# The small unit of the first feed-forward half step as a plain product with k outermost, PSUM banks of the units swapped, and the rotary angle tables computed in thirty short pieces

## The chip, the core and the metric

The kernel is one program on one core of a Trainium2 chip. The metric is the device time of one execution in microseconds (us), the median of several runs. TensorE (PE) multiplies, VectorE (DVE) and ScalarE (ACT) do elementwise work, GpSimd (POOL) a little of it, and SyncE (SP) issues the DMAs. Each engine works through its own instructions in the order of the program; between engines there are only semaphores.

## What is computed

Two layers, each of a feed-forward half step, a mixing block (attention and pooling) and a second feed-forward half step, on 512 tokens of 1024 channels in float32, then a final norm:

```python
def swiglu(h, w_gate, w_up, w_down):
    return (jax.nn.silu(h @ w_gate) * (h @ w_up)) @ w_down      # 1024 -> 2816 -> 1024

for l in range(2):
    x = x + 0.5 * swiglu(rmsnorm(x, ffn1_norm[l]), ffn1_w_gate[l], ffn1_w_up[l], ffn1_w_down[l])
    ...                                                          # mixing block with partial rotary attention
    x = x + 0.5 * swiglu(rmsnorm(x, ffn2_norm[l]), ffn2_w_gate[l], ffn2_w_up[l], ffn2_w_down[l])
return rmsnorm(x, final_norm)
```

The rotary part needs a table of cosines and sines of the positions, once for the whole program.

## The kernel before, in words

The residual x lies transposed in eight tiles x0 to x7 of 128 channels by 512 tokens; "chunk c" is tile c. Every float32 operand of a product is split into a high part (made by ACT as a rounded copy) and a low part (made by DVE as the difference), and each product is three matmuls: high by high, low by high, high by low. For the weights these parts are called `whi` and `wlo` (L357, L360), for chunk c of the normed input `ah` and `al` (L433, L434 for chunks 0 to 3, L439, L446 for 4 to 7).

A feed-forward half step (`ffn`) works through six units of its 2816 hidden channels: `UNITS = (5, 0, 1, 2, 3, 4)`, a small one of 256 channels first, then five large ones of 512. Of each unit `products` computes gate and up, and one unit later `down` multiplies the result into x. The gate and up product of a unit is done by a seven-product scheme on 2 by 2 blocks (`PORD = (1, 2, 6, 5, 7, 3, 4)`): instead of eight block products there are seven, in return for sums of weight blocks on DVE (`total`, `across`, `every`; L254, L258, L262, L266), sums of the outputs (`evacuate`), and sums and differences of input blocks (`fold`, L447 to L450, split in L453 to L458). Products 1, 2 and 4 take the input blocks themselves, products 6, 5, 7 and 3 the sums. For the small unit a matmul has 256 columns (168 matmuls), for a large one 512.

The order around the change is written by hand. `take` hands out the split weights of a step ("job") and first emits the split of the job two ahead, `divide`. `flush` emits the DVE halves that were put off. At the start, `startup` folds the eight chunks as they arrive and splits the first weights; the squares for the norm are emitted inside products 1 and 2 of the small unit (L662). Later norms come by `Norm.chunk`, called after each output tile of the last `down` or of the mixing block's residual (L937), which folds and squares it. `finish_col` closes a norm: four matmuls with a column of ones (L495), one DVE instruction, one power on POOL (L498). Then `activation_block` applies the gate (ACT L592, DVE L593).

PSUM has eight banks, two each under the tags A, B, C and D. In unit number n of a half step (n counts from 0, the small unit is n = 0) the tiles `px` take tag "AB"[n % 2] and the tiles `pz` the other. `down` uses C, transposes and norms use D. The mixing block's last output tiles, d = 0 to 7, take "AABBCCAA"[d].

The rotary tables are a generator, `tables` (L149). In the first half step of the first layer it is advanced once after each step numbered 6 or later of units n = 1 and n = 2 (L683), in seven pieces, all of which fall into n = 1.

Of the kernel before, what the change touches and what calls it, by code (L numbers as in the profile page):

```python
# [16 lines left out]
P = 128  # L17
# [61 lines left out]
def trunk(ctx: ExitStack, tc: tile.TileContext, a: dict):  # L79
# [39 lines left out]
    def startup(norm):  # L119
# [8 lines left out]
        for c in range(1, 4):  # L128
            nc.sync.dma_start(x[c], a["xT"][c])
        load()  # L130
        for c in range(4, KD):
            nc.sync.dma_start(x[c], a["xT"][c])
        pump()
        nc.sync.dma_start(ident, a["ident"])
# [6 lines left out]
        for c in range(KD):  # L141
            norm.fold(c)
            if c < 2:
                divide(c)
            if c == 4:
                divide()
            flush()

    def tables():  # L149
# [11 lines left out]
        def reduce(t):  # L161
            nearest(k, t, 1.0 / TWO_PI)
            for c in (C1, C2, C3):
                add_times(t, k, -c)
# [3 lines left out]
        nc.vector.tensor_scalar(ang, ang, col[:, 0:1], None, op0=ALU.mult)  # L168
        nearest(far, ang, 2.0**-17)
        add_times(ang, far, -2.0**17)  # L170
        yield
        reduce(ang)
        yield
        turn = t2([P, S], F32, "turn")
        nc.vector.tensor_scalar(turn, far, M1, None, op0=ALU.mult)
        reduce(turn)
        yield
        add_times(turn, far, M2)
        add_times(turn, far, M3)
        reduce(turn)  # L180
        yield
        nc.vector.tensor_tensor(ang, ang, turn, op=ALU.add)
        reduce(ang)
# [6 lines left out]
        nc.vector.tensor_tensor(k, k, k, op=ALU.mult)  # L190
        nc.vector.tensor_scalar(cosT, k, -2.0, 1.0, op0=ALU.mult, op1=ALU.add)
# [109 lines left out]
    def ffn_jobs(i, l):  # L301
        for n, u in enumerate(UNITS):
            pj = product_jobs(i, l, u)
# [105 lines left out]
    class Norm:  # L409
# [11 lines left out]
        def fold(self, c):  # L421

            H = S // 2
            if c == 0:
                self.xs, self.ah, self.al, self.sh, self.sl = ([None] * 4 for _ in range(5))
# [3 lines left out]
            if c < 4:  # L429
# [5 lines left out]
                                                             op=ALU.subtract))  # L435
                return
# [27 lines left out]
        def block(self, p, c, i):  # L464
# [5 lines left out]
            return tuple(t[c][:, z, i * P:(i + 1) * P] for t in (hi, lo))  # L470

# [112 lines left out]
    def ffn(which, l, norm, nxt, first=False):  # L584
# [20 lines left out]
        def products(n, u):  # L605
            N = S if u < NU else S // 2
            w, cps = N // 2, 2 if u < NU else 1
            xs = [bank("AB"[n % 2], f"px_{nm}_{u}_{i}") for i in range(2)]
# [485 lines left out]
```

## Time and profile before

| | before |
|---|---|
| median of 3 runs | 1922.75 us (1921.74 to 1922.85) |
| profiled execution, its own time | 1919.58 us |
| its span in the profile | 1917.8 us |
| TensorE busy | 1857.2 us (97% of the span) |
| VectorE busy | 1444.4 us (75%) |
| ScalarE busy | 950.4 us (50%) |
| GpSimd busy | 116.9 us (6%) |
| DMA | mean 101 GB/s |

TensorE is busy nearly all the time, so what can be won lies in its 60 us of idle time and in the stretches in which its clock is at the lower level. A busy share is a mean over stages with different limits; the stages that the change touches are the start, the first three large units of the first layer, and the three later places where a half step begins. The page's slices show TensorE below nine tenths only in the first three of forty.

### The profile page before, as it was taken

Reading aid. Unit: us, or ns where it says so; the run is one execution under the profiler, and the core shown is the slowest. Engines: PE = TensorE matmul, PEld = TensorE weight load, DVE = VectorE, ACT = ScalarE, POOL = GpSimd, SP = SyncE. Lnnn points to the kernel's source line nnn. Section 1 sums busy time; section 2 is a strip of 40 time slices with the busy share of each in tenths; the row PEclk is TensorE's granted clock in tenths of the full one; section 3 lists DMA queues with packets and bytes.
Section 4 is the critical chain, followed back from the end, with each engine's and each line's share of the span. In section 5 each row is a group of like instructions: output and inputs, shape, how many; then the busy total and the mean of one; then the engine's idle time right before and its main releaser. Section 6 shows DMA issues by size and latency. Waiting matters only on the chain.

```text
span 1917.8 us, 23563 instructions
## 1 busy us (share of the span) xinstructions
PE 1857.2 (97%) x8966; PEld 1551.3 (81%) x8966; DVE 1444.4 (75%) x2041; ACT 950.4 (50%) x1474; POOL 116.9 (6%) x105
## 2 busy tenths in 40 slices
PE   6989999999999999999989999999999989999998
PEld 5868888898877888888878888888888778888887
DVE  6996677647887986778688777675688688777675
ACT  6444344436665553444464444444476565444444
POOL 0000000013230000000000000000323200000000
PEclk7999999999999999999999999999999999999999
DMA  5223333125451233422313322340454223232321
GB/s 183 88 79 100 128 110 107 64 76 145 113 158 56 66 121 99 132 96 97 105 50 116 121 88 88 99 148 17 126 134 126 89 94 116 99 99 96 102 77 45
DMA packets 59696, 194.36 MB, mean 101 GB/s; under 512 B 7920, under 2 KB 8064, under 8 KB 59584
## 3 DMA queue, kind: packets, MB, share of 16 engines
q1 hardware_dynamic: 59440, 192.57, 31.9%
q8 instruction: 70, 1.15, 0.2%
q0 software_dynamic: 144, 0.29, 0.1%
q14 instruction: 42, 0.34, 0.1%
HBM read 171.87 MB, written 2.10 MB: 91 GB/s over the span
## 4 chain that ended last, share of the span: by engine, by line
PE 86%; DVE 8%; ACT 2%; issue 2%; DMA 1%; POOL 1%; SPq 0%; DVEq 0%; POOLq 0%; ACTq 0%
PE pd_f L384 8%; PE pd_f L383 8%; PE pd_f L382 8%; PE px_f L658 8%; PE px_f L655 8%; PE px_f L657 8%; PE pz_f L655 6%; PE pz_f L658 6%; PE pz_f L657 6%; PE pv_m L747 3%; PE ps_m L814 2%; PE pt_m L827 2%; PE pt_f L600 2%; DVE wlo L360 1%; PE po_m L843 1%
## 5 line engine op out<-in xcount | busy, mean ns | idle before, releaser
L360 DVE TENSOR_TENSOR wlo<-raw,whi 128x1024 fp32r<-128x1024 f32 (+2 forms) x421 | 502.0, 1198 | 55.4 <-ACT whi L357 50.4
L357 ACT ACTIVATE whi<-raw 128x1024 fp32r<-128x1024 f32 (+2 forms) x421 | 421.7, 1026 | 220.3 <-DVE wlo L360 63.9
L384 PE MATMUL pd_f<-ah_f,wlo 128*128 128x512 f32 (+1 forms) x736 | 282.2, 383 | 3.1 <-DVE wlo L360 3.1
L382 PE MATMUL pd_f<-ah_f,whi 128*128 128x512 f32 (+1 forms) x736 | 281.5, 382 | 1.0 <-ACT ah_f L400 1.0
L383 PE MATMUL pd_f<-al_f,whi 128*128 128x512 f32 (+1 forms) x736 | 280.7, 381 | 1.0 <-DVE al_f L403 1.0
L708 DVE SCALAR_TENSOR_TENSOR x<-pd_f,x 128x512 f32<-128x512 f32 x184 | 127.0, 690 | 168.8 <-PE pd_f L384 165.5
L592 ACT ACTIVATE c_f<-c_f,rcol_n 128x256 f32<-128x256 f32 (+1 forms) x144 | 70.3, 492 | 272.4 <-DVE c_f L637 102.5
L384 PEld LDWEIGHTS pd_f<-ah_f,wlo 128*128 128x128 f32 x736 | 138.7, 188 | 33.5 <-DVE wlo L360 7.7
L383 PEld LDWEIGHTS pd_f<-al_f,whi 128*128 128x128 f32 x736 | 138.8, 189 | 28.8 <-DVE al_f L403 2.3
L655 PE MATMUL px_f<-whi,ah_n 128*128 128x512 f32 (+1 forms) x384 | 145.9, 380 | 15.7 <-DVE x L937 11.5
L382 PEld LDWEIGHTS pd_f<-ah_f,whi 128*128 128x128 f32 x736 | 138.9, 189 | 27.4 <-ACT ah_f L400 1.9
L655 PE MATMUL px_f<-whi,sh_n 128*128 128x512 f32 (+1 forms) x384 | 144.1, 375 | 5.7 <-ACT c_f L622 5.7
L658 PE MATMUL px_f<-wlo,ah_n 128*128 128x512 f32 (+1 forms) x384 | 145.2, 378 | 1.2 <-DVE wlo L360 1.2
L658 PE MATMUL px_f<-wlo,sh_n 128*128 128x512 f32 (+1 forms) x384 | 144.1, 375 | 1.9 <-DVE wlo L360 1.9
L658 PE MATMUL pz_f<-wlo,sh_n 128*128 128x512 f32 (+1 forms) x384 | 143.3, 373 | 2.1 <-DVE wlo L360 2.1
L657 PE MATMUL px_f<-whi,al_n 128*128 128x512 f32 (+1 forms) x384 | 145.3, 378 | 0.0
L655 PE MATMUL pz_f<-whi,sh_n 128*128 128x512 f32 (+1 forms) x384 | 143.7, 374 | 0.6 <-DVE c_f L624 0.3
L657 PE MATMUL px_f<-whi,sl_n 128*128 128x512 f32 (+1 forms) x384 | 143.7, 374 | 0.0
L657 PE MATMUL pz_f<-whi,sl_n 128*128 128x512 f32 (+1 forms) x384 | 143.1, 373 | 0.0
L819 ACT ACTIVATE e_m<-e_m,nmx_m 128x512 f32<-128x512 f32 x96 | 69.4, 723 | 78.7 <-DVE nmx_m L817 78.1
L655 PEld LDWEIGHTS px_f<-whi,ah_n 128*128 128x128 f32 x384 | 74.3, 193 | 30.1 <-DVE x L937 11.9
L817 DVE CUSTOM_DVE_ANT_0 e_m<-ps_m,gbias 128x512 f32<-128x512 f32 x96 | 65.9, 686 | 33.8 <-PE ps_m L814 33.3
(206 smaller groups left out, 3580.4 us busy)
## 6 DMA issues: line engine op xcount, KB each, us to landing
raw<-in_gu SPq DMA_DIRECT2D x160, 512.0 KB, 3.3
raw<-in_dn SPq DMA_DIRECT2D x80, 512.0 KB, 3.3
raw<-in_wqk SPq DMA_DIRECT2D x24, 512.0 KB, 5.4
qq_m<-hl_q_m SPq DMA_DIRECT2D x48, 256.0 KB, 4.2
raw<-in_wo SPq DMA_DIRECT2D x16, 512.0 KB, 5.3
raw<-in_gs SPq DMA_DIRECT2D x15, 512.0 KB, 4.9
raw<-in_wv SPq DMA_DIRECT2D x16, 384.0 KB, 3.1
kk_m<-hl_k_m SPq DMA_DIRECT2D x48, 128.0 KB, 2.3
```

Of the source, the lines that this page charges most:

```text
L357: nc.scalar.activation(hi[:, o:e], raw[:, o:e], AF.Copy)
L360: nc.vector.tensor_tensor(lo[:, o:e], raw[:, o:e], hi[:, o:e].bitcast(F32), op=ALU.subtract)
L382: nc.tensor.matmul(ps, hi[:, o:o + P], act[0], start=start, stop=False)
L383: nc.tensor.matmul(ps, hi[:, o:o + P], act[1], start=False, stop=False)
L384: nc.tensor.matmul(ps, lo[:, o:o + P], act[0], start=False, stop=stop)
L592: nc.scalar.activation(c[:, :w], src[:, :w], AF.Silu, scale=r)
L655: nc.tensor.matmul(ps, bh, hi[:, o], start=(k == 0 and p in (1, 2, 5)), stop=False, skip_group_check=True)
L657: nc.tensor.matmul(ps, bl, hi[:, o], start=False, stop=False, skip_group_check=True)
L658: nc.tensor.matmul(ps, bh, lo[:, o], start=False, stop=(k == 3), skip_group_check=True)
L708: nc.vector.scalar_tensor_tensor(x[d], ps, 0.5, x[d], op0=ALU.mult, op1=ALU.add)
L817: nc.vector.tensor_tensor_reduce(e, ps, gbias[:, o:o + S], -0.125, 3.0e38, ALU.add, ALU.min, nmx[hd][:, it:it + 1])
L819: nc.scalar.activation(e, e, AF.Exp, bias=nmx[hd][:, it:it + 1], scale=-1.0, accum_out=den[hd][:, it:it + 1])
```

## The change

The gate and up product of the small unit (n = 0) of the first half step, in both layers, becomes a plain product: a new function `plain_unit` with four PSUM tiles of 128 tokens (tags A, A, B, B), input chunk k outermost, 512 columns per matmul, 96 matmuls. Its weights come as four plain jobs of two k slices each. `Norm.fold` makes two more parts, `a2`, of the second half of chunks 0 to 3 for it (one ACT and one DVE instruction of 256 columns each). The bank tags of units are swapped in all half steps. At the start the loads are put in the order in which k needs them, and the squares are emitted in the fold loop. The tables yield after nearly every DVE instruction or pair, and are advanced after every step from number 2 on of n = 1, 2 and 3.

```diff
-        for c in range(1, 4):
+        nc.sync.dma_start(x[1], a["xT"][1])
+        nc.sync.dma_start(x[2], a["xT"][2])
+        load(2)
+        nc.sync.dma_start(x[3], a["xT"][3])
+        for c in range(4, KD):
+            if c % 2 == 0:
+                load()
             nc.sync.dma_start(x[c], a["xT"][c])
...
         for c in range(KD):
             norm.fold(c)
-            if c < 2:
-                divide(c)
-            if c == 4:
-                divide()
+            if c < 4:
+                divide(c % 2)
             flush()
+            if c > 0:
+                norm.square(c - 1)
+        norm.square(KD - 1)
...
         def reduce(t):
             nearest(k, t, 1.0 / TWO_PI)
-            for c in (C1, C2, C3):
-                add_times(t, k, -c)
+            yield
+            add_times(t, k, -C1)
+            yield
+            add_times(t, k, -C2)
+            yield
+            add_times(t, k, -C3)
+            yield
...
     def ffn_jobs(i, l):
         for n, u in enumerate(UNITS):
+            if i == 1 and u == NU:
+                for g in range(4):
+                    plain(("c", l, g), a["gc"][l, g], D)
+                continue
...
+                if self.n % 3 == 0:
+                    a2 = t2([P, 2, H], F32R, f"a2_{nm}")
+                    self.a2[k] = a2
+                    nc.scalar.activation(a2[:, 0, :], xs[:, 1, :], AF.Copy)
+                    later.append(lambda: nc.vector.tensor_tensor(a2[:, 1, :], xs[:, 1, :], a2[:, 0, :].bitcast(F32),
+                                                                 op=ALU.subtract))
...
-            xs = [bank("AB"[n % 2], f"px_{nm}_{u}_{i}") for i in range(2)]
+            xs = [bank("BA"[n % 2], f"px_{nm}_{u}_{i}") for i in range(2)]
...
-                    zs.update({i: bank("BA"[n % 2], f"pz{p}_{nm}_{u}_{i}") for i in range(2)})
+                    zs.update({i: bank("AB"[n % 2], f"pz{p}_{nm}_{u}_{i}") for i in range(2)})
...
-                    if first and not n and p in (1, 2):
-                        for k in range(4 * p - 4, 4 * p):
-                            norm.square(k)
-                            flush()
...
-                    if first and n in (1, 2) and z >= 6:
+                    if first and n in (1, 2, 3) and z >= 2:
                         next(rotary, None)
...
+        def plain_unit(u):
+
+            ps = [bank("AABB"[t], f"pc_{nm}_{t}") for t in range(4)]
+
+            def part(t, k, w, o):
+                ah, al = norm.tile_of(t, k)
+                hi, lo = (v[:, o:o + S] for v in w)
+                nc.tensor.matmul(ps[t], ah, hi, start=(k == 0), stop=False)
+                nc.tensor.matmul(ps[t], al, hi, start=False, stop=False)
+                nc.tensor.matmul(ps[t], ah, lo, start=False, stop=(k == KD - 1))
+
+            for g in range(3):
+                flush()
+                w = take("c", l, g)
+                for z in range(2):
+                    for t in range(4):
+                        part(t, 2 * g + z, w, z * S)
+                    flush()
+            w = take("c", l, 3)
+            norm.finish_col()
+            cs = [t2([P, S], F32, f"cc_{nm}_{t}") for t in range(4)]
+            for t in range(4):
+                for z in range(2):
+                    part(t, 6 + z, w, z * S)
+                flush()
+                activation_block(cs[t], ps[t], t, S // 2)
+            for j in range(2):
+                turns.append(lambda j=j: turn(u, j, cs, j, S // 2))
...
-            products(n, u)
+            if n == 0 and which == 1:
+                plain_unit(u)
+            else:
+                products(n, u)
```

The first place is VectorE at the start. Of the names, `al_n_3` is the low part of chunks 3 and 7, `s_n` and `sl_n` are the sums of the seven-product scheme and their low parts, `sq_n` the squares of the norm, `wlo` the low parts of weights. After the change, from the last fold on, its instructions stand so:

```order
39 L469 TENSOR_TENSOR al_n_3_175<-xs_n_7_236,ah_n_3_174 128x512
40 L470 TENSOR_TENSOR s_n_7_239<-xs_n_3_172,xs_n_7_236 128x256
41 L471 TENSOR_TENSOR s_n_7_240<-s_n_7_239,xs_n_3_172 128x256
42 L472 TENSOR_TENSOR s_n_7_239<-xs_n_3_172 128x256
43 L473 TENSOR_TENSOR s_n_7_240<-xs_n_7_236,s_n_7_240 128x256
44 L480 TENSOR_TENSOR sl_n_6_223<-s_n_6_221,sh_n_6_222 128x512
45 L481 TENSOR_TENSOR sl_n_6_223<-s_n_6_220,sh_n_6_222 128x512
46 L512 TENSOR_TENSOR sq_n_0_155<-sq_n_0_155,sq_n_5_234 128x512
47 L480 TENSOR_TENSOR sl_n_7_242<-s_n_7_240,sh_n_7_241 128x512
48 L481 TENSOR_TENSOR sl_n_7_242<-s_n_7_239,sh_n_7_241 128x512
49 L512 TENSOR_TENSOR sq_n_0_155<-sq_n_0_155,sq_n_6_253 128x512
50 L512 TENSOR_TENSOR sq_n_0_155<-sq_n_0_155,sq_n_7_255 128x512
```

Directly behind these come the low parts of the third and fourth weight job of the plain unit (k = 4 to 7), which TensorE needs next, and two more:

```order
51 L377 TENSOR_TENSOR wlo_267<-raw_99,whi_266 128x1024
52 L377 TENSOR_TENSOR wlo_303<-raw_103,whi_302 128x1024
53 L377 TENSOR_TENSOR wlo_333<-raw_108,whi_332 128x1024
54 L377 TENSOR_TENSOR wlo_363<-raw_110,whi_362 128x1024
55 L529 TENSOR_SCALAR rcol_n_371<-ms_n_366 128x4
```

Before the change the same stretch of VectorE held sums of weight blocks, and the squares came after the folds:

```order
30 L446 TENSOR_TENSOR al_n_3_155<-xs_n_7_204,ah_n_3_154 128x512
31 L447 TENSOR_TENSOR s_n_7_207<-xs_n_3_152,xs_n_7_204 128x256
32 L448 TENSOR_TENSOR s_n_7_208<-s_n_7_207,xs_n_3_152 128x256
33 L449 TENSOR_TENSOR s_n_7_207<-xs_n_3_152 128x256
34 L450 TENSOR_TENSOR s_n_7_208<-xs_n_7_204,s_n_7_208 128x256
35 L457 TENSOR_TENSOR sl_n_6_194<-s_n_6_192,sh_n_6_193 128x512
36 L458 TENSOR_TENSOR sl_n_6_194<-s_n_6_191,sh_n_6_193 128x512
37 L254 TENSOR_TENSOR raw_84<-raw_84,raw_102 128x1024
38 L258 TENSOR_TENSOR sum_5_0_227<-raw_84,raw_104 128x1024
39 L457 TENSOR_TENSOR sl_n_7_210<-s_n_7_208,sh_n_7_209 128x512
40 L458 TENSOR_TENSOR sl_n_7_210<-s_n_7_207,sh_n_7_209 128x512
41 L360 TENSOR_TENSOR wlo_230<-sum_5_0_227,whi_229 128x1024
```

The squares have moved in among the folds, the weight sums are gone, and the weights of k = 4 to 7 stand behind the whole of both.

The second place is VectorE in the first large unit of the first layer (n = 1), around the low parts of the weights of steps 5 and later (`wlo`; x is written by `down`). Before the change a reduction stood as one block (`kmul`, `ang`):

```order
101 L360 TENSOR_TENSOR wlo_704<-raw_279,whi_703 128x1024
102 L708 SCALAR_TENSOR_TENSOR x_66<-pd_f_5_2_731,x_66 128x512
103 L360 TENSOR_TENSOR wlo_727<-raw_371,whi_726 128x1024
104 L708 SCALAR_TENSOR_TENSOR x_67<-pd_f_5_3_740,x_67 128x512
105 L155 TENSOR_SCALAR kmul<-ang 128x512
106 L156 TENSOR_SCALAR kmul<-kmul 128x512
107 L159 SCALAR_TENSOR_TENSOR ang<-kmul,ang 128x512 x3
108 L360 TENSOR_TENSOR wlo_754<-raw_615,whi_753 128x512
```

After the change the first pieces stand between earlier weight splits, one at a time (`far` is a table tile too):

```order
68 L377 TENSOR_TENSOR wlo_470<-sum_0_0_432,whi_469 128x1024
69 L279 TENSOR_TENSOR raw_112<-raw_112,sum_0_0_432 128x1024
70 L176 CAST ang<-pos_i 128x512
71 L177 TENSOR_SCALAR ang<-ang,col 128x512
72 L377 TENSOR_TENSOR wlo_497<-sum_0_1_473,whi_496 128x1024
73 L279 TENSOR_TENSOR raw_114<-raw_114,sum_0_1_473 128x1024
74 L656 TENSOR_TENSOR c_f_0_0_447<-pz_f_0_0_475,c_f_0_0_447 128x512
75 L656 TENSOR_TENSOR c_f_0_1_449<-pz_f_0_1_476,c_f_0_1_449 128x512
76 L159 TENSOR_SCALAR far<-ang 128x512
77 L160 TENSOR_SCALAR far<-far 128x512
78 L377 TENSOR_TENSOR wlo_520<-raw_335,whi_519 128x512
79 L163 SCALAR_TENSOR_TENSOR ang<-far,ang 128x512
```

Two pieces now stand ahead of the split of the first `down` weights (`wlo_520`), where before none did; by the end of this unit twelve pieces are done, and the rest follows in n = 2 and n = 3.

## Rows read from the trace of the kernel before

**Rows 1.** Chain that ended last: transposes opening each unit (start us, us, what).
```profile
60.65 0.87 PE pt_f L600 x8
...
120.40 0.88 PE pt_f L600 x8
...
1006.76 0.87 PE pt_f L600 x8
...
1056.66 0.87 PE pt_f L600 x8
```
**Rows 2.** Timeline, TensorE: where units begin (start us, us, engine, line, what).
```profile
55.02 0.40 PE L655 MATMUL px_f<-whi,ah_n 128*128 128x512 f32 x1
...
968.84 0.28 PE L655 MATMUL px_f<-whi,ah_n 128*128 128x256 f32 x1
...
1001.13 0.40 PE L655 MATMUL px_f<-whi,ah_n 128*128 128x512 f32 x1
```
**Rows 3.** Stretches: us, busy us (instructions) of PE, PEld, DVE, ACT, POOL; PEclk.
```profile
46.38:55.02 8.64, 8.64 (x75) 8.64 (x73) 6.13 (x12) 5.00 (x9) 0.00 (x0) 1.00 0.12 31
55.02:60.49 5.47, 5.47 (x27) 4.46 (x25) 5.22 (x7) 2.86 (x4) 0.00 (x0) 1.00 0.02 3
103.73:106.29 2.56, 2.56 (x8) 1.98 (x6) 2.42 (x5) 0.00 (x0) 0.00 (x0) 0.50 0.00 0
624.85:628.47 3.62, 3.62 (x18) 3.62 (x18) 3.59 (x9) 1.56 (x4) 0.00 (x0) 0.50 0.00 0
20.51:23.78 3.27, 1.23 (x3) 0.79 (x3) 3.23 (x8) 2.39 (x5) 0.00 (x0) 0.60 0.56 213
```
**Rows 4.** Timeline, ScalarE at the start: one chunk, the next, chunk 4, squares.
```profile
8.81 0.72 ACT L428 ACTIVATE xs_n<-x,vecs 128x512 f32<-128x512 f32 x1 [1.34 <-DMA x<-in_xT]
...
9.57 0.42 ACT L433 ACTIVATE ah_n<-xs_n 128x256 fp32r<-128x256 f32 x1
...
9.89 0.61 ACT L357 ACTIVATE whi<-raw 128x512 fp32r<-128x512 f32 x1
...
10.41 0.71 ACT L428 ACTIVATE xs_n<-x,vecs 128x512 f32<-128x512 f32 x1
...
12.61 0.72 ACT L428 ACTIVATE xs_n<-x,vecs 128x512 f32<-128x512 f32 x1
...
30.53 2.17 ACT L474 ACTIVATE sq_n<-x 128x512 f32<-128x512 f32 x4
```
**Rows 5.** Timeline, VectorE: chunk 4's low part, a weight sum, table pieces, a split.
```profile
14.03 0.69 DVE L446 TENSOR_TENSOR al_n<-xs_n,ah_n 128x512 fp32r<-128x512 f32 x1 [0.94 <-ACT ah_n L439]
...
968.95 1.22 DVE L254 TENSOR_TENSOR raw<-raw,raw 128x1024 f32<-128x1024 f32 x1
...
86.18 2.15 DVE L159 SCALAR_TENSOR_TENSOR ang<-kmul,ang 128x512 f32<-128x512 f32 x3
...
1017.76 0.68 DVE L360 TENSOR_TENSOR wlo<-raw,whi 128x512 fp32r<-128x512 f32 x1
```
**Rows 6.** Chain that ended last: the norm's four products on TensorE, one square sum.
```profile
41.00 1.28 PE ms_n L495 x8
...
610.80 0.60 DVE sq_n L480
```
**Rows 7.** Timeline, TensorE after waits: restart, then the clock's rise; a first down step.
```profile
103.14 0.79 PE L384 MATMUL pd_f<-ah_f,wlo 128*128 128x512 f32 x1 [2.62 <-DVE wlo L360]
...
106.63 0.40 PE L383 MATMUL pd_f<-al_f,whi 128*128 128x512 f32 x1
...
624.47 0.58 PE L655 MATMUL px_f<-whi,ah_n 128*128 128x256 f32 x1 [5.76 <-DVE x L937]
...
628.85 0.28 PE L658 MATMUL pz_f<-wlo,ah_n 128*128 128x256 f32 x1
...
631.79 0.39 PE L658 MATMUL px_f<-wlo,sh_n 128*128 128x256 f32 x1 [0.35 <-DVE wlo L360]
...
1018.42 0.39 PE L382 MATMUL pd_f<-ah_f,whi 128*128 128x512 f32 x1
```

More of the change, by code (lines that the diff above doesn't have):

```diff
@@ L127, in startup @@
         nc.scalar.activation(npow, npow, AF.Copy)
-        for c in range(1, 4):
+        nc.sync.dma_start(x[1], a["xT"][1])
[5 more added lines that the diff above has]
+                load()
             nc.sync.dma_start(x[c], a["xT"][c])
-        load()
-        for c in range(4, KD):
-            nc.sync.dma_start(x[c], a["xT"][c])
+        nc.sync.dma_start(ident, a["ident"])
         pump()
-        nc.sync.dma_start(ident, a["ident"])
         pos = a["positions"]
@@ L162, in reduce @@
             nearest(k, t, 1.0 / TWO_PI)
-            for c in (C1, C2, C3):
-                add_times(t, k, -c)
+            yield
[5 more added lines that the diff above has]
+            yield
         nc.vector.tensor_copy(ang, pos_i)
         nc.vector.tensor_scalar(ang, ang, col[:, 0:1], None, op0=ALU.mult)
+        yield
         nearest(far, ang, 2.0**-17)
+        yield
         add_times(ang, far, -2.0**17)
         yield
-        reduce(ang)
-        yield
+        yield from reduce(ang)
         turn = t2([P, S], F32, "turn")
         nc.vector.tensor_scalar(turn, far, M1, None, op0=ALU.mult)
-        reduce(turn)
         yield
+        yield from reduce(turn)
         add_times(turn, far, M2)
+        yield
         add_times(turn, far, M3)
-        reduce(turn)
         yield
+        yield from reduce(turn)
         nc.vector.tensor_tensor(ang, ang, turn, op=ALU.add)
-        reduce(ang)
+        yield
+        yield from reduce(ang)
         pif = float(np.float32(3.1415925))
@@ L190, in tables @@
         nc.vector.tensor_tensor(k, k, k, op=ALU.mult)
+        yield
         nc.vector.tensor_scalar(cosT, k, -2.0, 1.0, op0=ALU.mult, op1=ALU.add)
@@ L424, in fold @@
             if c == 0:
-                self.xs, self.ah, self.al, self.sh, self.sl = ([None] * 4 for _ in range(5))
+                self.xs, self.ah, self.al, self.sh, self.sl, self.a2 = ([None] * 4 for _ in range(6))
             k, nm = c % 4, f"{self.name}_{c}"
@@ L470, in block, with tile_of @@
             return tuple(t[c][:, z, i * P:(i + 1) * P] for t in (hi, lo))
+        def tile_of(self, t, c):
+            if t >= 2 and c < 4:
+                both = (self.a2[c][:, 0, :], self.a2[c][:, 1, :])
+            else:
+                z = 0 if c < 4 else 1 if t < 2 else 2
+                both = (self.ah[c % 4][:, z, :], self.al[c % 4][:, z, :])
+            return tuple(v[:, t % 2 * P:(t % 2 + 1) * P] for v in both)
         def square(self, c):
@@ L713, in ffn @@
         for n, u in enumerate(UNITS):
-            products(n, u)
+            if n == 0 and which == 1:
+                plain_unit(u)
+            else:
+                products(n, u)
             if first and n == 3:
@@ L1057 @@
         arrays[f"gu{i}"] = big.transpose(0, 6, 1, 7, 2, 4, 3, 5, 8).reshape(L, NU, 2, 2, 2, P, D)
-        small = pair[..., NB:].reshape(L, 2, 4, P, 2, 2, P)
-        arrays[f"gs{i}"] = small.transpose(0, 1, 5, 3, 2, 4, 6).reshape(L, 2, 2, P, D)
+        small = pair[..., NB:]
+        if i == 1:
+            arrays["gc"] = small.reshape(L, 4, 2, P, S).transpose(0, 1, 3, 2, 4).reshape(L, 4, P, D)
+        else:
+            arrays["gs2"] = small.reshape(L, 2, 4, P, 2, 2, P).transpose(0, 1, 5, 3, 2, 4, 6).reshape(L, 2, 2, P, D)
         dn = v[f"ffn{i}_w_down"]
```

## The prediction

> **What bounds the kernel now.** I read the page first: TensorE is busy 97% of the span, so a gain has to come from its 60 us of idle time or from stretches at the lower clock. Then the waits of TensorE by stretch, which put nearly all of that into four places: the start, the first large unit (n = 1) of the first layer, and the three later starts of a half step. There I read the timelines. The reader is to see three things.
>
> At the start TensorE works in bursts, its granted clock is 0.60 of full in the mean of one such stretch, between the levels of 1.2 and 2.4 GHz [rows 3], and it reaches the first large unit at 55.02 us [rows 2]. In the first large unit VectorE is the bound: from its opening transposes to the next unit's it takes 120.40 - 60.65 = 59.75 us, the same unit without tables 1056.66 - 1006.76 = 49.90 us in layer two [rows 1]. At the starts of the second half steps TensorE waits 5.76 us for the residual add that frees its bank, but the wait at 631.79 is for a weight split on VectorE [rows 7], and the chain that ended last runs through VectorE up to there.
>
> **Prices.** A matmul of 512 columns takes 5.47 / 24 = 0.228 us at the full clock and 2.56 / 6 = 0.427 at the lower, one of 256 columns 8.64 / 72 = 0.120 and 3.62 / 17 = 0.213 [rows 3] (24, 6, 72 and 17 begin in these stretches, the counts shown include neighbours). So a microsecond at the lower clock loses 0.47 us with 512 columns, 0.44 with 256. After a wait the clock came back 106.63 - 103.14 = 3.5 and 628.85 - 624.47 = 4.4 us after the restart [rows 7]; I take 4.2, that is 2.0 us lost by each restart of 512-column work. The plain unit alone has more to do: 96 x 0.228 = 21.9 us against 168 x 0.120 = 20.2, 1.7 us more. It gains only where TensorE was waiting, so I work out the end of each unit.
>
> The Trainium skill (TensorE: Matmul & The Clock Gate, "Back-to-back issue gap") gives an isolated gap of N/2.4 + 2.5 ns, 109 and 216 ns here. By it the plain unit would cost 96 x 0.216 - 168 x 0.109 = 2.4 us more instead of 1.7; the rows are above the page for both shapes, and I use the rows.
>
> **The start.** On ScalarE a chunk now holds xs 0.76, ah 0.32, the new a2 (as ah) 0.32, half a weight split 0.52, and a square of the chunk before at about 0.52 (four in 2.1): 2.44 us [rows 4]. Chunk 1 begins when its load lands, 8.81 as before, since what is queued ahead of it on SP is unchanged in size; the later loads have several us in hand. So chunk 4 begins at 8.81 + 3 x 2.44 = 16.13, and its low part on VectorE 14.03 - 12.61 = 1.42 later, at 17.55 instead of 14.03 [rows 4, 5]. From there VectorE is never idle: four chunks at 3.27 (13.1) [rows 3] and six square sums at 0.60 (3.6) [rows 6] end at 34.2. Only then, as the order shows, comes the split for k = 4 and 5, at 1.2 like the weight sum of the same shape [rows 5]: 35.4.
>
> The first 48 matmuls, k = 0 to 3, need 10.9 to 20.5 us and can begin by 8 us, so they lie under this chain wholly, with 7 us to spare even at the lower clock. Then TensorE stands still, and from 35.4 has 46 left (two of the second 48 need only the high part): 46 x 0.228 = 10.5, the norm's products 1.2 [rows 6], the restart 2.0. It ends at 49.1 against 55.02: **5.9 us gained**. The norm's small chain (DVE, POOL, then the gates on ACT) has the last 24 matmuls as its cover; were that cover gone, it would cost some 2 us. Bounds: 7.9 if the clock stays up, 4.4 if the chain of ACT and VectorE is 1.5 us longer.
>
> **The tables.** What n = 1 lost to them is 59.75 - 49.90 = 9.85 us. Not all comes back. A piece takes about 0.7 us (2.15 for three) to 0.95 [rows 5]. In layer two the split for the first down step ended at 1018.44 and was needed at 1018.42 + 2 x 0.228 = 1018.88 [rows 5, 7]: 0.44 us in hand, and two pieces, 1.9 us, now stand ahead of it. So TensorE waits 1.5 us there, and I add 0.2 for the piece after. Twelve pieces, some 9 us, fall into n = 1; the later ones meet splits that are made further ahead. In n = 2 and 3 the same step is again preceded by two pieces and one: 1.0 us for both, an estimate from the same rows. **7.1 us gained**; bounds 9.85 (every piece hidden) and 4.5 (the waits doubled).
>
> **Layer two, first half step.** Two weight sums that began at 968.95 [rows 5] go. What stands on VectorE from there to the third weight job: two residual adds, eight low parts of sums, three square sums and two al, 15 x 0.60 = 9.0; two groups of four short sums, 3.27 - 3 x 0.60 = 1.5 each; one split 1.2: 13.1, to 982.1, then the split for k = 4, 5: 983.2. The a2 parts come earlier, in gaps that VectorE had there. TensorE begins at 968.84 [rows 2] and has done k = 0 to 3 at 979.8, so it waits 3.4 us, about as long as the wait that ended at 103.14, after which the clock was down. Then 10.5 + 1.2 + 2.0: 996.9 against 1001.13 [rows 2], **4.2 us gained**; bounds 6.2 (clock stays up) and 2.5.
>
> **The bank swap.** It removes the 5.76 us wait at both second half steps, since px then takes the B banks, read much earlier. But what is late next is unchanged: product 2 needs the low part of chunk 7, which VectorE makes at about 626.8, and product 6 its split at 631.79 [rows 7]. The twelve matmuls only move ahead of the wait. Some 14 remain after 626.8, 3.0 us at 0.213, then a pause until 631.79. Before, the clock had risen at 628.85; now its rise may come only after 631.79, with TensorE the bound from there: 3 to 4.4 us at 0.44. Between 0 and 2.5 us lost at each; I take 1.5, **3.0 us lost**. Elsewhere the swapped banks are free long before their next use; plain_unit's A banks are read while its last tiles are multiplied.
>
> **Sum.** 5.9 + 7.1 + 4.2 - 3.0 = 14.2 us. The profiled execution took 1919.58 us, 3.2 below the median of 1922.75; it would take 1905.4. On the median: **1908.5 us**.
>
> **Rivals.** (a) All covers hold: no clock falls at the plain units, no piece is late, the swap is free: 7.9 + 9.85 + 6.2 = 24 us, 1899. For it: VectorE has idle time later in n = 1. Against it: the margin of 0.44 us and the waits of 3 us and more. (b) The plain unit gains nothing: k = 4 to 7 run at the lower clock throughout, 46 x 0.427 = 19.6, ending at 56.2 and 1004.0: 1.2 and 2.9 us lost, the tables' 7.1 less the swap's 3.0 remain: about 1922.75. Against it: both restarts in rows 7 regained the clock within 4.4 us.
>
> (c) Slower: at the two swapped starts TensorE now works in short bursts, and the clock stays down for the rest of the small unit: 120 matmuls x 0.093 = 11.2 us each instead of 1.5. That gives 17.2 - 22.3 = -5.1, so 1928. It decides the sign once the clock stays down for more than 90 matmuls. Against it: from 631.79 on work is dense. A rule stands on its side: the Trainium skill (same page, "HAM oscillation — how this bites in real kernels") says that waits between bursts bring TensorE back to half rate each time; the trace agrees that it falls (624.47), and also that it comes back once work is dense.
>
> (d) The pieces all end on the path: 27 x 0.72 = 19.4 us late instead of 9.85, so -9.6 in place of +7.1: 1925, no change to slightly slower. Against it: margins grow after the first down step.
>
> **Chances.** Forecast with its bounds (1901 to 1916) 0.68; (a) 0.14; between forecast and no change 0.08; (b) 0.04; (c) 0.03; (d) 0.03. Range 1899 to 1916, which leaves out (b) to (d) and what is beyond. Faster by over 0.2% (about 3.9 us, what a measurement here can tell from no change) 0.89, within it 0.07, slower 0.04.
>
> **What would show it.** The first 512-column matmul of unit 0 at about 49 with a pause of TensorE from some 20 to 35 us; the opening transposes of n = 1 and n = 2 about 51.6 us apart; unit 0 of layer two begun 28.1 instead of 32.3 us after the last down step; at the second half steps no wait on the residual, but one on chunk 7's low part of about 5 us, and a low clock after it. It is wrong if the weights of k = 4 to 7 are ready before 30 us, if tables stall n = 2 by over 2 us, or if a buffer that the longer-lived table tiles hold makes another engine wait.

## The result, and the profile after the change

The changed kernel takes **1903.65 us** (median of 4 runs, 1900.74 to 1906.05) against 1922.8 us of the kernel before on the same chip: ratio 0.9898, 95% interval 0.9880 to 0.9915, some 19 us faster. Forecast were 1908.5 us, range 1899 to 1916. The profiled execution took 1906.05 us, the slowest of the four, where that of before (1919.58) was faster than all its other runs. So the two profiles differ by less than the medians do: 13.9 us of span.

The page of the changed kernel: its span, and TensorE's busy time (us, share, instructions), which was 1857.2 us before.

```profile
span 1903.9 us, 23219 instructions
PE 1854.1 (97%) x8822; PEld 1542.4 (81%) x8822; DVE 1422.6 (75%) x2016; ACT 942.6 (50%) x1457; POOL 117.0 (6%) x105
```

**The start.** Timeline of TensorE (start us, us, engine, line, what, and in brackets the wait before it and who ended it). The weights of k = 4 restart it after 12.71 us, their low part after another 2.12; a record then shows 0.63 with starts 0.43 apart, the lower clock, until 42.82; unit 0 begins at 51.09 where it began at 55.02 [rows 2], and the transposes of n = 1 at 56.53.

```profile
33.34 0.80 PE L735 MATMUL pc_f<-whi,ah_n 128*128 128x512 f32 x1 [12.71 <-ACT whi L374]
...
36.68 0.79 PE L737 MATMUL pc_f<-wlo,ah_n 128*128 128x512 f32 x1 [2.12 <-DVE wlo L377]
37.27 0.63 PE L735 MATMUL pc_f<-whi,ah_n 128*128 128x512 f32 x1
...
42.82 0.43 PE L736 MATMUL pc_f<-whi,al_n 128*128 128x512 f32 x1
...
51.09 0.39 PE L687 MATMUL px_f<-whi,ah_n 128*128 128x512 f32 x1
...
56.53 1.04 PE L632 MATMUL pt_f<-ident,cc_f 128*128 128x128 f32 x8
```

VectorE in the same stretch: two square sums, and directly behind them, as the order showed, the four splits, the first of them those of k = 4 and 5.

```profile
34.09 1.41 DVE L512 TENSOR_TENSOR sq_n<-sq_n,sq_n 128x512 f32<-128x512 f32 x2
35.41 4.62 DVE L377 TENSOR_TENSOR wlo<-raw,whi 128x1024 fp32r<-128x1024 f32 x4
```

**Units.** The chain that ended last: opening transposes of n = 2, 3 and 4, and of n = 1 in layer two, the places of [rows 1].

```profile
107.50 0.87 PE pt_f L632 x8
...
170.47 0.87 PE pt_f L632 x8
...
232.88 0.88 PE pt_f L632 x8
...
991.99 0.87 PE pt_f L632 x8
```

In TensorE's own timeline, where the transposes of n = 2 stand at 107.34, n = 1 now takes 107.34 - 56.53 = 50.81 us (59.75 before), n = 2 62.97, n = 3 62.41. The pieces' price is seen at the first down step of n = 1 and n = 2, the step of [rows 7]:

```profile
69.58 0.50 PE L401 MATMUL pd_f<-ah_f,wlo 128*128 128x512 f32 x1 [0.62 <-DVE wlo L377]
...
121.66 0.50 PE L401 MATMUL pd_f<-ah_f,wlo 128*128 128x512 f32 x1 [0.98 <-DVE wlo L377]
```

**A swapped start** (second half step, layer one). The 5.76 us on the residual [rows 7] are gone; 3.49 us for the low part of a weight split stand in their place, chunk 7's parts follow, and the lower clock (records of 0.41 us, starts 0.21 apart with 256 columns) stays until 623.2:

```profile
611.30 0.38 PE L690 MATMUL pz_f<-wlo,ah_n 128*128 128x256 f32 x1 [3.49 <-DVE wlo L377]
...
613.32 0.58 PE L687 MATMUL pz_f<-whi,ah_n 128*128 128x256 f32 x1 [0.93 <-ACT ah_n L462]
614.30 0.58 PE L689 MATMUL pz_f<-whi,al_n 128*128 128x256 f32 x1 [0.41 <-DVE al_n L469]
...
622.80 0.41 PE L687 MATMUL px_f<-whi,sh_n 128*128 128x256 f32 x1
...
623.20 0.28 PE L690 MATMUL px_f<-wlo,sh_n 128*128 128x256 f32 x1
```

### The profile page after: what moved, and what is told of

The parts are those of the page before. It is cut to its first block, busy times and chain, and to the rows that moved or that the text cites. A ratio compares the mean times of both kernels' runs of the same rounds, so it can differ in the third digit from the quotient of the medians.

```text
span 1903.9 us, 23219 instructions
## 1 busy us (share of the span) xinstructions
PE 1854.1 (97%) x8822; PEld 1542.4 (81%) x8822; DVE 1422.6 (75%) x2016; ACT 942.6 (50%) x1457; POOL 117.0 (6%) x105
## 4 chain that ended last, share of the span: by engine, by line
PE 89%; DVE 7%; ACT 2%; issue 1%; DMA 0%; SPq 0%; DVEq 0%; POOLq 0%; POOL 0%; ACTq 0%
PE pd_f L401 8%; PE pd_f L400 8%; PE pd_f L399 8%; PE px_f L690 8%; PE px_f L687 8%; PE px_f L689 8%; PE pz_f L687 6%; PE pz_f L690 6%; PE pz_f L689 6%; PE pv_m L807 4%; PE ps_m L874 2%; PE pt_m L887 2%; PE pt_f L632 2%; DVE wlo L377 1%; PE pp_q_m L399 1%
## 5 line engine op out<-in xcount | busy, mean ns | idle before, releaser
L687 PE MATMUL px_f<-whi,sh_n 128*128 128x512 f32 (+1 forms) x352 | 135.6, 385 | 1.4 <-ACT c_f L654 1.4
L690 PE MATMUL px_f<-wlo,sh_n 128*128 128x512 f32 (+1 forms) x352 | 135.3, 384 | 0.1
L689 PE MATMUL px_f<-whi,sl_n 128*128 128x512 f32 (+1 forms) x352 | 135.1, 384 | 0.0
L687 PE MATMUL pz_f<-whi,sh_n 128*128 128x512 f32 (+1 forms) x352 | 133.7, 380 | 0.0
L690 PE MATMUL px_f<-wlo,ah_n 128*128 128x512 f32 (+1 forms) x352 | 133.6, 380 | 0.0
L689 PE MATMUL px_f<-whi,al_n 128*128 128x512 f32 (+1 forms) x352 | 133.6, 379 | 0.0
L687 PE MATMUL px_f<-whi,ah_n 128*128 128x512 f32 (+1 forms) x352 | 133.6, 379 | 0.0
L690 PE MATMUL pz_f<-wlo,sh_n 128*128 128x512 f32 (+1 forms) x352 | 133.5, 379 | 0.0
L689 PE MATMUL pz_f<-whi,sl_n 128*128 128x512 f32 (+1 forms) x352 | 133.5, 379 | 0.0
L530 POOL TENSOR_TENSOR rcol_n<-rcol_n,npow 128x4 f32<-128x4 f32 x6 | 6.1, 1016 | 1238.2 <-DVE rcol_n L529 1238.2
```

The costliest lines, as they stand in the source:

```text
L687: nc.tensor.matmul(ps, bh, hi[:, o], start=(k == 0 and p in (1, 2, 5)), stop=False, skip_group_check=True)
L689: nc.tensor.matmul(ps, bl, hi[:, o], start=False, stop=False, skip_group_check=True)
L690: nc.tensor.matmul(ps, bh, lo[:, o], start=False, stop=(k == 3), skip_group_check=True)
```

## The experiments

All are made from the changed kernel, and none leaves out a part of the computation. The diffs are excerpts, with the changed kernel on the minus side; remarks behind # are added here. Each time stands beside runs of the kernel before on the same chip; a ratio is to these. Where a profile is compared by place, times are TensorE's own timeline.

**1. Both kernels once more**, for a second profile of each.

> The changed kernel itself once more, as the measure for the runs beside it. The four times of it on hand spread from 1900.74 to 1906.05 us, those of the kernel before from 1921.74 to 1925.43, with a profiled execution of 1919.58. Theory 1: the gain is about 14 to 15 us in every pair of executions, as the two profiles show it place by place (start 3.9, tables 7.9, layer two 3.5, swap -2.6), and the 19 us between the medians are chance: the ratio over five rounds comes to 0.9925, some 14.5 us. Theory 2: the profiled execution of the kernel before was a lucky one at the start, and the gain is 19 us, ratio 0.990, most of the additional 5 us within the first 60 us.

> The kernel before once more, for a second profile of it. Its profiled execution on hand took 1919.58 us, its other executions 1920.73 to 1925.43. Theory: the spread of both kernels comes from how TensorE's clock falls and rises at the few places where it waits (the start and the three later starts of a half step), so the second profile agrees with the first within 0.1 us everywhere else, and differs by 1 to 3 us at one or more of these four places. Rival: the difference lies in the loads at the start, and nothing behind 61 us differs.

Measured: the changed kernel 1902.82 us (1899.25 to 1904.78), ratio 0.9897 [0.9882, 0.9912], its profile a span of 1898.9; the kernel before 1921.63 us (ratio to the other runs of it 0.9995 [0.9985, 1.0006]), its profile 1919.5. The gain of 19 to 20 us is real, and the small one of the first pair of profiles was chance, as theory 2 has it; but of the 6.7 us that the second pair shows more, 2.0 lie at the start and 4.1 in layer two, so theory 2 had the place wrong. By place, in us won (first pair: the two profiles at hand; second pair: the two new ones):

| place | forecast | first pair | second pair |
|---|---|---|---|
| start, to the first transposes of n = 1 | 5.9 | 4.0 | 6.0 |
| tables, n = 1 to 4 | 7.1 | 7.8 | 7.9 |
| layer two, first half step | 4.2 | 3.5 | 7.6 |
| bank swap, both sites | -3.0 | -1.4, -1.2 | -1.2, 0.0 |
| all else | 0 | 1.2 | 0.2 |
| span | 14.2 | 13.9 | 20.6 |

So the profiles of one kernel differ mainly at the places where TensorE waits: the two of the kernel before by 0.9 us at the start and 1.3 in layer two, not at all at the second half steps, but also by 0.2 in n = 1 and in n = 2 and by some 0.5 between the opening of n = 5 and layer one's second half step, which is more than the 0.1 expected. In layer two's plain unit one sees what differs. First the changed kernel's first profile, then its second; the waits are the same to 0.01 us:

```profile
970.00 0.50 PE L735 MATMUL pc_f<-whi,ah_n 128*128 128x512 f32 x1 [1.41 <-ACT whi L374]
...
972.02 0.80 PE L737 MATMUL pc_f<-wlo,ah_n 128*128 128x512 f32 x1 [1.28 <-DVE wlo L377]
972.61 0.63 PE L735 MATMUL pc_f<-whi,ah_n 128*128 128x512 f32 x1
...
978.15 0.40 PE L736 MATMUL pc_f<-whi,al_n 128*128 128x512 f32 x1
```

```profile
968.70 0.50 PE L735 MATMUL pc_f<-whi,ah_n 128*128 128x512 f32 x1 [1.41 <-ACT whi L374]
...
970.73 0.50 PE L737 MATMUL pc_f<-wlo,ah_n 128*128 128x512 f32 x1 [1.29 <-DVE wlo L377]
971.06 0.39 PE L735 MATMUL pc_f<-whi,ah_n 128*128 128x512 f32 x1
```

In the first the clock fell and came back 6.1 us later (978.15 - 972.02), in the second it never fell. Over the eight profiles in which this unit stood as changed, from the last transposes before it to those behind it took 55.12 to 55.15 us four times, and 56.68, 57.91, 57.93 and 58.01.

**2. The bank swap undone.**

```diff
-            xs = [bank("BA"[n % 2], ...
+            xs = [bank("AB"[n % 2], ...          # pz the other way round
-            ps = [bank("AABB"[t], f"pc_{nm}_{t}") for t in range(4)]
+            ps = [bank("BBAA"[t], f"pc_{nm}_{t}") for t in range(4)]
```

> The bank tags of units are put back as before the change (the small plain unit with B, B, A, A accordingly); everything else as changed. Theory (the term of the prediction): the swap only moves twelve matmuls ahead of a wait that stays, and delays the clock's rise; it cost 1.4 and 1.2 us at the two second half steps by the profiles, so without it 2.6 us are won against the changed kernel run beside it (bounds 1.5 to 4), with a wait of 5.8 us on the residual add back in the trace. Rival: the freed wait of 5.76 us at each site is worth its size or part of it, and the loss seen there has another cause: 2 to 11 us slower than the changed kernel.

Measured: 1902.11 us (1901.05 to 1902.36), ratio 0.9892 [0.9878, 0.9905]: 0.7 us below the changed kernel, less than its runs spread and less than the 1.5 us expected at least, but with a spread of 1.3 instead of 5.5 us. So the medians do not show a loss by the swap. The place tells more. Timeline of TensorE at the layer-one site without the swap; one pause of 5.77 us, full clock again (0.28) at 615.25, before product 6 begins at 617.80:

```profile
611.32 0.58 PE L687 MATMUL px_f<-whi,ah_n 128*128 128x256 f32 x1 [5.77 <-DVE x L997]
...
615.25 0.28 PE L687 MATMUL pz_f<-whi,ah_n 128*128 128x256 f32 x1
...
617.80 0.39 PE L687 MATMUL px_f<-whi,sh_n 128*128 128x256 f32 x1 [0.23 <-ACT c_f L654]
```

From the small unit's first matmul to the transposes behind it took 35.54 to 35.58 us at all ten sites without the swap (five profiles: before twice, this one, experiments 6 and 8). At the eighteen with it (nine profiles) it took 35.56 or 35.57 eight times, and 36.56 to 37.20 ten times: seven of nine in layer one, three of nine in layer two, 1.0 and 0.4 us in the mean. At all eighteen the lower clock is seen 2.0 us behind the restart; what decides is when the upper one comes back: by 7.1 us behind it, ahead of the weight split that sets the end, where nothing is lost, and 10.7 to 12.1 us behind it where something is. Mostly this goes with the time of the fall. At the nine sites where it came only behind the restart, as at 613.32 above, all lost; at the nine where the restart was slow already, eight lost nothing, as in the second profile, layer two:

```profile
1539.71 0.58 PE L690 MATMUL pz_f<-wlo,ah_n 128*128 128x256 f32 x1 [3.49 <-DVE wlo L377]
...
1546.79 0.38 PE L687 MATMUL px_f<-whi,sh_n 128*128 128x256 f32 x1 [0.71 <-ACT c_f L654]
1547.01 0.28 PE L689 MATMUL px_f<-whi,sl_n 128*128 128x256 f32 x1
```

The ninth is layer one's site in experiment 6: slow at the restart too, yet back latest of all, and the dearest (37.20 us):

```profile
604.15 0.58 PE L697 MATMUL pz_f<-wlo,ah_n 128*128 128x256 f32 x1 [3.49 <-DVE wlo L376]
...
616.48 0.28 PE L696 MATMUL px_f<-whi,sl_n 128*128 128x256 f32 x1
```

The rival (the freed wait is worth something) has no case: no swapped site was shorter than 35.56.

**3. The tables in seven pieces again.** The generator's yields stand where they stood before the change, and:

```diff
-                    if first and n in (1, 2, 3) and z >= 2:
+                    if first and n in (1, 2) and z >= 6:
```

> The angle tables are again computed in seven pieces in the first large unit, after its steps from number 6 on; everything else as changed. Theory: the pieces keep VectorE from the weight splits in that unit; 9.85 us are lost there again and 2 us of waits in the units behind are saved, so 7.5 to 8 us slower than the changed kernel (bounds 5 to 9), and the opening transposes of units n = 1 and n = 2 stand 59 to 60 us apart instead of 51.0. Rival: the plain small unit has changed the state in which VectorE enters the first large unit (it arrives with less in arrears), so the old tables would cost less there now: under 4 us slower.

Measured: 1907.63 us (1906.19 to 1910.18), ratio 0.9924 [0.9911, 0.9936], 4.8 us above the changed kernel run beside it. The chain that ended last shows n = 1 back at 60 us, 115.85 - 55.84:

```profile
55.84 0.87 PE pt_f L623 x8
...
115.85 0.88 PE pt_f L623 x8
```

From there to the opening of n = 5 it takes 245.76 us, the kernel before to the hundredth the same (306.41 - 60.65), the changed kernel 237.96: 7.8 us. By place the rival (under 4 us) is refuted. By the medians it is 4.8, below the 5 us expected at least; both kernels' clocks fell at other places by chance (this one's profile had none of it in layer two), and five executions do not settle how much of the 3 us that is.

**4. The plain unit in layer one only.** 
```diff
-            if i == 1 and u == NU:
+            if i == 1 and l == 0 and u == NU:
...
-            if n == 0 and which == 1:
+            if n == 0 and which == 1 and l == 0:
```

> The small unit of layer two's first half step is again the seven-product scheme of 256 columns; layer one keeps the plain unit. Theory: the plain unit there gains by being less hungry for VectorE (no weight sums ahead of the split for k = 4 and 5), although it has 1.7 us more of multiplying to do; 3.5 us slower without it (2.5 to 4.5), with the distance from the last down step to unit 0 back at about 32 us. Rival: the gain in that place in the profile came from the bank swap or from the order of a2 parts, not from the plain product: within 1 us of the changed kernel.

Measured: 1908.08 us (1906.07 to 1908.95), ratio 0.9923 [0.9909, 0.9936]: 5.3 us slower, more than expected. By place the unit takes 62.65 us, in the kernel before 61.48 and 62.76, against 55.1 to 58.0 with the plain unit (the parts `a2`, made for it alone, go with it). So it is the plain product that gains there, not the swap, and its size depends on whether the clock falls.

**5. The start as before.** Loads, first splits, squares and the seven-product scheme of layer one's small unit are put back; layer two keeps the plain unit.

```diff
-            if n == 0 and which == 1:
+            if n == 0 and which == 1 and l == 1:
...
+                    if first and not n and p in (1, 2):
+                        for k in range(4 * p - 4, 4 * p):
+                            norm.square(k)
+                            flush()
```

> Changed kernel, but with the start of the kernel before: the small unit of layer one by the seven-product scheme, the loads, the first splits and the squares where they were. Layer two keeps the plain unit. Theory: the opening transposes of n = 1 come at 60.5 to 61.5 us, as in the two profiles of the kernel before, instead of 54.8 to 56.5 in seven profiles with the changed start, and the time is 5 to 6 us above the changed kernel's 1902.8: 1908 to 1909. Rival: the first large unit had taken part of the start's gain back (VectorE being its bound), so that less than 3 us are lost.

Measured: 1908.19 us (1907.31 to 1909.62), ratio 0.9925 [0.9912, 0.9939], 5.4 us slower. The transposes of n = 1 come at 61.98 us, n = 1 then takes 50.83, so it had taken nothing back. Loads, splits, squares and the plain product are put back together here, so how much each of them is worth is not shown:

```profile
61.98 1.04 PE L628 MATMUL pt_f<-ident,c_f 128*128 128x128 f32 x8
```

The four undoings together give 4.8 + 5.3 + 5.4 - 0.7 = 14.8 us of the 19 to 20. The interval of each ratio, and of the changed kernel's, reaches 2.4 to 2.9 us to either side, so what is missing is no proof of an interplay; it stays open.

**6. What sets the pause at the start: the splits first.**

```diff
         for c in range(KD):
-            norm.fold(c)
-            if c < 4:
-                divide(c % 2)
+            norm.fold(c, held)        # sums of chunks 4 to 7 are put by
+            divide(c % 2)
             flush()
 ...                                   # plain_unit, behind each of its last four tiles:
+                if held:
+                    sums, parts, rests = held.pop(0)
...
```

> Changed kernel; at the start the weights of k = 4 to 7 are split one half with each of chunks 4 to 7, directly behind their low parts, and the sums of input blocks (four sums and two low parts per chunk) are put off until the last tiles of the plain unit. Nothing is left out. Theory: TensorE's pause of 12 us at the start is VectorE's work on those sums ahead of the splits; with the splits first k = 4 to 7 follow k = 0 to 3 with no pause over 2 us, and unit 0 begins at 33 to 37 instead of 50 us. VectorE, which was idle for 14 us between 11 and 106 us, stays the bound to the end of n = 1, so part is given back there: the opening transposes of n = 2 come 6 to 10 us earlier than at 106.4, the time is 1893 to 1897. Rival: the pause is set by the loads or by ScalarE, or the sums are then missed so badly in n = 1 that all is given back: within 2 us of the changed kernel.

Measured: 1893.15 us (1892.49 to 1899.25), ratio 0.9842 [0.9824, 0.9859], against 0.9897 for the changed kernel: some 10 us faster. Timeline of TensorE: the pause of 12 us is gone, k = 0 to 5 run through, a wait of 2.93 us for the norm's last square sum is left ahead of the last tiles (the clock falls on it), and unit 0 begins at 38.65 (expected 33 to 37) instead of 50.

```profile
28.98 1.58 PE L534 MATMUL ms_n<-ones,sq_n 128*128 128x1 f32 x8 [2.93 <-DVE sq_n L519]
30.43 0.77 PE L742 MATMUL pc_f<-whi,ah_n 128*128 128x512 f32 x1
...
36.12 0.42 PE L743 MATMUL pc_f<-whi,al_n 128*128 128x512 f32 x1
...
38.65 0.39 PE L694 MATMUL px_f<-whi,ah_n 128*128 128x512 f32 x1
```

About half of these 11 us is given back: the transposes of n = 2 come at 100.16, 6.1 us earlier. (What the medians show beyond that is not seen in the profile, whose execution, 1899.25 us, had a fallen clock at all three later starts.) VectorE has become the bound in the first part of n = 1, where TensorE is busy for 10.65 of 14 us; from 60 us on TensorE is busy for 39.33 of 40 again. Columns: stretch, length, busy us (instructions) of PE, PEld, DVE, ACT, POOL, granted clock, DMA share, GB/s.

```profile
46.00:60.00 14.00, 10.65 (x43) 7.62 (x43) 13.90 (x16) 4.95 (x8) 0.00 (x0) 1.00 0.14 38
60.00:100.00 40.00, 39.33 (x174) 32.24 (x173) 38.11 (x56) 20.07 (x28) 0.00 (x0) 1.00 0.40 125
```

**7. The tables later.**

```diff
-                    if first and n in (1, 2, 3) and z >= 2:
+                    if first and n in (2, 3, 4, 5) and z >= 6:
```

> Changed kernel, with the thirty table pieces advanced after steps from number 6 on of units n = 2 to 5 instead of from number 2 on of n = 1 to 3. Theory (the prediction's margin): a piece costs only where a weight split has less than a piece in hand, that is around the first down steps; away from them it costs nothing. So n = 1 goes from 51.0 to 49.9 us, n = 2 from 63.0 to 61.8, n = 3 from 62.4 to 61.8, and n = 4 and 5 stay at 61.8: 2.5 to 3 us faster. Rival: VectorE is so full in the large units that a piece costs a part of itself wherever it stands: no gain.

Measured: 1898.76 us (1896.13 to 1901.54), ratio 0.9872 [0.9853, 0.9892]: 4.1 us below the changed kernel by the medians, 4.8 by the ratios, whose intervals overlap. By place the theory holds to 0.1 us: n = 1 takes 49.87 us and n = 2 to 4 take 61.78, 61.75 and 61.79, each as long as a unit without tables; 2.8 us in all. The chain that ended last, opening transposes of n = 3, 4 and 5:

```profile
167.84 0.87 PE pt_f L632 x8
...
229.59 0.87 PE pt_f L632 x8
...
291.38 0.88 PE pt_f L632 x8
```

**8. Layer two's waits: its sums later.** The sums of chunks 6 and 7 alone are put by, as in experiment 6, and nothing else.

```diff
-                self.fold(c)
+                self.fold(c, held if self.n == 3 and c >= 6 else None)
```

> Changed kernel; in layer two's first half step alone the sums of input blocks of chunks 6 and 7 (5.4 us of VectorE) are put off until the last tiles of the plain unit. Nothing is left out. Theory: TensorE's two waits in that plain unit (1.41 us for the high part, 1.28 us for the low part of the weights of k = 4 and 5) are VectorE's and ScalarE's work on these sums; they go, and with them the fall of the clock that followed them in some executions (0, 1.2 or 2.8 us in four profiles). The opening transposes of n = 0 stand 58.5 to 59.0 us after the last transposes of the half step before, instead of 61.5, 63.0 or 64.3, and the time falls from about 1902.8 to 1898 to 1899.5. Rival: the sums are missed in the next unit instead (its product 6 needs them) and the two waits come back there: 1902 or more.

Measured: 1897.46 us (1895.83 to 1898.16), ratio 0.9869 [0.9855, 0.9882], 5.4 us below the changed kernel. From the last transposes but one before the unit to those behind it (a longer stretch than in experiments 1 and 4) it takes 58.22 us (926.63 to 984.85 in the chain) against 61.48 and 64.28, the next unit is no longer for it (49.85 us in all three), and TensorE is busy without a gap at the full clock, where the changed kernel's two profiles, shown first, had waited, the first with a fallen clock (same columns):

```profile
968.00:979.00 11.00, 8.31 (x23) 5.98 (x22) 7.37 (x9) 4.90 (x6) 0.00 (x0) 0.69 0.10 25
```

```profile
968.00:979.00 11.00, 9.01 (x42) 7.28 (x43) 6.32 (x9) 4.08 (x5) 1.01 (x1) 1.00 0.07 25
```

```profile
968.00:979.00 11.00, 11.00 (x54) 9.21 (x53) 5.66 (x14) 2.99 (x7) 1.12 (x1) 1.00 0.00 0
```

**9. Put together.** First experiments 2, 6 and 7; then with 8; then with 8 but the swapped tags.

> The early splits, the later tables and the old bank tags together. Theory: with nine us of table pieces out of n = 1, VectorE's work up to the end of n = 1 falls to about 76 us, so the opening transposes of n = 2 come at 88 to 92 us instead of 106.4; n = 2 and 3 win 1.8 us, the missing swap about 1: 1882 to 1889 us. Rival: TensorE then waits in many short stretches in n = 1, its clock falls at each, and the sum is no better than the parts alone, 1893 or more.

> Early splits, later tables, old bank tags and the later sums in layer two together. Theory: the parts add up, since they stand in different places: 1890.2 less the 2.7 to 5.5 us of layer two's plain unit, 1885 to 1888 us. Rival: what is won in layer two is only the chance of the clock, and the median stays at 1889 to 1891.

> The kernel with everything together, 1884.83 us (1884.26 to 1885.91), with the changed kernel's bank tags in place of the old ones. Theory: the small unit of a second half step takes 35.56 us with the old tags in all ten places seen; with the swapped tags 35.57 or 36.6 to 37.2, by chance of the clock, in layer one mostly the longer: 0.5 to 2.5 us slower and a wider spread. Rival: the swap also has a good side (banks free earlier at the plain units) that was not visible beside the tables: same or faster.

Measured: 1890.24 us (1887.71 to 1891.94), ratio 0.9827 [0.9809, 0.9844]; with layer two's sums later **1884.83 us** (1884.26 to 1885.91), ratio 0.9804 [0.9791, 0.9818]; with the swap 1887.9 us (1886.04 to 1888.23), ratio 0.9817 [0.9803, 0.9830]. The first missed its expectation: the transposes of n = 2 come at 96.94, not at 88 to 92. I had counted VectorE's work alone; but TensorE itself needs 49.87 us behind its first transposes, which come at 41.34, and it loses 5.7 more there: 3.3 in three waits early in n = 1, and the clock is down behind them. The second gained 5.4 us by the medians, as in experiment 8 alone, 4.4 by the ratios. It beats both kernels, by 2.0% and 1%, and its spread is 1.65 us. Its page, and its chain at n = 2:

```profile
span 1883.9 us, 23225 instructions
PE 1848.4 (98%) x8822; PEld 1540.3 (82%) x8822; DVE 1422.3 (75%) x2018; ACT 941.2 (50%) x1459; POOL 117.1 (6%) x105
```

```profile
97.70 0.87 PE pt_f L639 x8
```

The swap costs it 2.5 us by the ratios, whose intervals overlap, and 3.1 by the medians. The profile shows 1.3 of that at layer one's site (36.84 us against 35.55) and 0.8 at the start, where the clock came back 2 us later, which can be chance.

## Why the prediction was right, and where its sizes were off

The sign and the range held, and the tables were the largest term by place, as forecast; layer two and the start came out about equal. Step by step:

- **The start** (5.9 us). The mechanism held: VectorE works without a gap on folds, sums and squares, then come the splits; k = 0 to 3 lie under it; TensorE pauses. The splits ended their first part at about 36.6 instead of 35.4, because chunk 1 landed at 9.86 instead of 8.81 in that execution (9.26 in the second); and the upper clock came back 6.1 and 4.9 us behind that split, not 4.2. Unit 0 began at 51.09 and 49.95, forecast 49.1. Seven profiles with this start have the first transposes at 54.78 to 56.53, the kernel before at 60.49 and 61.42: 5.3 us in the mean. Experiment 6 shows the cause, by taking it away.
- **The tables** (7.1 us): 7.8 and 7.9 in the two pairs of profiles, 7.8 in experiment 3. The split that I put 1.5 us late was 0.62 late; the two pieces ahead of it took 0.86 and 0.79 us (63.72 to 64.58, 68.05 to 68.84) instead of 0.95, and the rest of that margin I did not trace. n = 2 and 3 paid 1.1 us more than before, as estimated (1.0). Experiment 7 shows the margin: away from the first down steps a piece costs nothing.
- **Layer two** (4.2 us): 3.5 to 7.6, 5.7 in the mean of eight profiles against two. This is the term that was mis-sized. I took a wait of 3.4 us and then the clock's fall, 2.0 us, as certain. The wait is 1.41 + 1.28 us, and after it the clock fell in four of eight profiles. I had read the row at 103.14 [rows 7] as a rule, from one case; and its 2.0 us rest on a return after 4.2 us, where it was 3 to 6.
- **The swap** (-3.0 us): -2.6, -1.2, and 1.4 in the mean of nine profiles. The mechanism held in the main: no wait on the residual, a wait for a low part, a low clock behind it. But the wait is for product 2's weight split, 3.49 us, not for chunk 7's low part, some 5 us; on VectorE that split stands directly ahead of the residual add (610.03 and 611.16), so what the swap freed came only some 0.6 us earlier. Chunk 7's parts follow with 0.93 and 0.41. And at eight of eighteen sites the clock came back in time, and the same split as before set the end. As in layer two, a loss that comes by chance was charged as if it came always.
- **The sum, and from the span to the median.** That 14.2 lies so near the 13.9 of the first pair of profiles is luck: that pair was the least favourable one, the kernel before 3.2 us below its median, the changed one 2.4 above. By the medians the gain is 19 us, and the means by place above add up to 5.3 + 7.8 + 5.7 - 1.4 = 17.4. So the sum was 3 us short by place, most of it layer two and the swap, and some 5 by the medians; what makes the rest no run here shows.

Of the rivals, (a) came nearest: in the second pair of profiles the covers of layer two did hold (7.6 us, above the 6.2 set for that), though the pause at the start did not go away. (b) is refuted by the clock's return at 42.82 and 978.15, ahead of the unit's end, (c) by the swapped sites, which lose 1.6 us at most instead of 11.2, (d) by n = 1 at 50.8. The rule on (c)'s side, in the Trainium skill (TensorE: Matmul & The Clock Gate, "HAM oscillation — how this bites in real kernels"), that waits between bursts bring TensorE back to half rate each time, is told there of waits of 3 to 5 us for loads. The traces agree for the 3.49 us wait, behind which the lower clock was seen at eighteen of eighteen sites; behind waits of 1.41 and 1.28 us it was seen in four of eight profiles, so for such short waits the rule cannot be taken as it stands. The same page, "Part 1: The HAM clock gate", says that the point of change varies from run to run for the same kernel; the traces agree (at the start, the upper clock 9.5 us behind the restart in one execution of the changed kernel and 8.2 in another).

## What to carry to other kernels

When a reordering leaves a bound engine's work in place, look at what the waiting engine needs next, and put that ahead of work which is needed later: here the four splits ahead of the sums were worth 6 us by place and 10 by the medians, and the regrouping of the start before that 5.3. Price a short wait of TensorE as two cases, with and without the clock's fall, and take a second profile before calling the one the rule. Small pieces of background work were free here away from the first down steps, where the splits are made further ahead (experiment 7), and cost TensorE 0.62 and 0.98 us at them.

## What the runs showed of the hardware

TensorE's clock answered differently to the same two waits, equal to 0.01 us, in eight executions of the changed kernel and of variants that leave this place alone: it stayed at the upper level in four, and was at the lower one for some 3 to 6 us in four others. After the long pause at the start it came back 8.2 to 9.5 us after the restart (33.34 to 42.82, 32.76 to 40.97), of which 2.1 were a second wait, where the kernel before had shown 3.5 and 4.4 us [rows 7]. Those two rows were themselves a draw: behind the one wait of 5.76 or 5.77 us, at the ten sites without the swap, it came back 3.1 to 6.1 us after the restart. At the second half steps, with the same wait of 3.49 us, eight swapped sites lost nothing and ten lost 1.0 to 1.6 us, by when the upper clock came back: a fall by the time of the restart was free at eight of nine sites, a later one at none of nine. What decides between them no run here shows.
